# Gate projections that leave PSUM by one copy, with their product on GpSimd

## The chip, the cores and the metric

The kernel runs on one core of a Trainium2 chip. Its five engines are TensorE (PE; its weight loads are listed as PEld), VectorE (DVE), ScalarE (ACT), GpSimd (POOL) and SyncE (SP), which issues nearly all DMAs here. Each engine works through its own queue in order and waits on semaphores of the others. The metric is the device time of one execution in microseconds; less is better.

## The reference

One encoder layer over two sequences (1024 and 256 tokens, 1280 in all, width 1024). A wide projection feeds three groups of heads: a bidirectional gated delta rule (6 heads), bidirectional retention (6 heads) and windowed attention (4 heads). The output of each group is multiplied by a gate, silu of a slice of the projection, and the result goes through an output projection and a gated embedding.

```python
xn = rms_norm(h, norm_g)
proj = jnp.matmul(xn, w_in).astype(f32)
(a_qkv, a_gate, a_beta, a_alpha, b_q, b_k, b_v, b_gate,
 c_q, c_k, c_v, c_gate) = jnp.split(proj, splits, axis=-1)
...
o_a = (rms_norm(o_fwd + o_bwd, dn_norm_g) * jax.nn.silu(heads(a_gate, A_HEADS))).reshape(b, t, A_WIDTH)
...
o_b = head_layer_norm(r, ret_norm_g.astype(f32)) * jax.nn.silu(b_gate)
o_c = window_attention(...) * jax.nn.silu(c_gate)
mix = jnp.concatenate([o_a, o_b, o_c], axis=-1).astype(h.dtype)
h = h + jnp.matmul(mix, w_out)
h = h + jnp.matmul(p_i, w_ple) * jax.nn.sigmoid(jnp.matmul(h, w_pg))
```

silu(z) is z times sigmoid(z). There are eight gate slices of 128 columns: 0 to 2 for the delta rule, 3 to 5 for retention, 6 and 7 for attention.

## The kernel before

Activations stand transposed (features on partitions, tokens along the free axis), each as a high and a low part (`xh`, `xl`), and so do weights (`whi`, `wlo`). A dense product of 128 columns (`dense`, line 170) is three matmuls per 128 rows of the contraction and 256 tokens; it runs in three blocks of 512, 512 and 256 tokens. Each block fills one PSUM tile `mm`, of which there are two, and is then emptied by an evacuation function. `load_w` (line 133) brings a product's weights by one DMA (`raw`), rounds them on ScalarE (`whi`, line 148) and subtracts on GpSimd (`wlo`); the weights of the next product are loaded while one runs.

After the normalisation and the convolution of the delta rule comes the preparation (`prep_stream`, line 564). It goes through the ten token blocks from the last to the first and makes two steps for each, one per direction: 20 steps. A step takes Gram matrices (`sa`) from `kq`, decay factors from VectorE (`gt`), two matmuls `sb`, exponentials on ScalarE (`ge`), and products on VectorE (`at`, `l2`) and GpSimd (`l2`). Each step stores `at` (to `agd` and `ad`) and `l2` (to `l2d`). There are two `at` buffers, and ScalarE's copy into `at` (line 603) waits for the earlier stores. After five blocks, and again after ten, `invert` loads `agd` into `ot`, inverts 120 triangular 32x32 blocks for both directions by 61 operations on VectorE (`ot<-ot`, 120 partitions), and stores them as `yd`.

Beside the preparation run eleven dense products in the order cq0, cq1, gate 6, 7, 3, 4, 0, 5, cv, gate 1, 2 (`PP`). For a gate, the evacuation `evg` (line 468) computes sigmoid by three activations on ScalarE (exponential of the negated PSUM block, logarithm with bias one, exponential), then VectorE multiplies by the PSUM block. Gates 6 and 7 stay in `ot`; the other six go to DRAM (`gd`) by a DMA on SP's queue and are read again much later.

```python
sg = o if n >= 6 else gp.tile([128, 512], F32, tag="sg", name=nm("sg"))[:, :w]
sigmoid(sg, pp[:, :w])
tt(V, sg, sg, pp[:, :w], MUL)
```

Next come the product ck (`kst`), windowed attention, the joins of the inverted blocks (`join`: loads `an` and `yn`, GpSimd makes `yc`), the scan over 20 chunks (`scan_stream`), retention, and from about 830 us on the output products. `bias` is attention's table of distances, made on VectorE and finished by two selections on GpSimd.

The order of instructions on each engine is set at build time: a scheduler replays the program on a modelled timeline and writes one list per engine. Evacuations and weight roundings have high priority there. Pools on the right side of SBUF are a stack: `wp` (weights), `gp` (gate tiles, two of `sg`), `pc` (constants), and after `pc` closes, `sc` and `inv` for the scan and the joins.

Of the kernel before, what the change touches and what calls it, by code (L numbers as in the profile page):

```python
# [8 lines left out]
F32 = mybir.dt.float32  # L9
# [43 lines left out]
def encoder_kernel(ctx: ExitStack, tc: tile.TileContext, I, O, dbg=None, upto=99):  # L53
# [3 lines left out]
    def nm(s):  # L57
        uid[0] += 1
        return f"{s}_{uid[0]}"
# [14 lines left out]
    wp_cm = tc.tile_pool(name="wp", bufs=2, side="right")  # L74
    wp = wp_cm.__enter__()
    gp_cm = tc.tile_pool(name="gp", bufs=2, side="right", reuse_waits="tile")
    gp = gp_cm.__enter__()
# [3 lines left out]
    def pt_(shape, name, dt=F32):  # L81
        return pc.tile(list(shape), dt, name=name)
# [4 lines left out]
    def tt(eng, out, a, b, op):  # L87
        eng.tensor_tensor(out=out, in0=a, in1=b, op=op)  # L88

    V, S, G = nc.vector, nc.scalar, nc.gpsimd  # L90
    MUL, ADD, SUB, MAX = ALU.mult, ALU.add, ALU.subtract, ALU.max
# [3 lines left out]
        name=nc.get_next_instruction_name(), act_func_set_id=ACT_SET, ins=[], outs=[]))  # L95

    def sigmoid(out, in_):

        S.activation(out=out, in_=in_, func=AF.Exp, scale=-1.0)
        S.activation(out=out, in_=out, func=AF.Ln, bias=one_c)  # L100
        S.activation(out=out, in_=out, func=AF.Exp, scale=-1.0)  # L101
# [85 lines left out]
    tmpp = tmp_cm.__enter__()  # L187
# [45 lines left out]
        return  # L233


    onesbd = pt_([128, 128], "onesbd")
    G.memset(onesbd, 0.0)
    for h in range(2):
        G.memset(onesbd[64 * h:64 * h + 64, 64 * h:64 * h + 64], 1.0)
# [12 lines left out]
    for d in range(2):  # L252
        sg = 1 if d == 0 else -1
# [130 lines left out]
    def plain(dst, eng=S, scale=None):  # L384
        def evac(p, t0, n):
            if scale is None:
                S.copy(dst[:, t0:t0 + n], p[:, :n])
            else:
                S.activation(out=dst[:, t0:t0 + n], in_=p[:, :n], func=AF.Copy, scale=scale)
        return evac  # L390
# [58 lines left out]
    def length(ns):  # L449
        return 12.8 * len(ns) or 1.0, prods(*ns)  # L450
# [15 lines left out]
    def product(n):  # L466
        if n in GCOL:
            def evg(pp, t0, w):
                o = ot[:, n, t0:t0 + w]
                sg = o if n >= 6 else gp.tile([128, 512], F32, tag="sg", name=nm("sg"))[:, :w]  # L470
                sigmoid(sg, pp[:, :w])
                tt(V, sg, sg, pp[:, :w], MUL)
                if n in GD:
                    nc.sync.dma_start(out=GD[n][:, t0:t0 + w], in_=sg)
                elif n < 3:
                    tt(V, o, o, sg, MUL)
            return [(GCOL[n], 128)], evg
        if n[0] == "c":

            return {"cq0": ([(3096, 64), (3224, 64)], plain(ot[:, 4, :], scale=cols[:, 54:55])),  # L480
                    "cq1": ([(3160, 64), (3288, 64)], plain(ot[:, 5, :], scale=cols[:, 55:56])),
                    "ck": ([(3352, 128)], evk),
                    "cv": ([(3480, 128)], plain(ot[:, 1, :]))}[n]
        p = int(n[1])
        col, dst = {"q": (1560, ot[:, 3 + p, :]), "k": (1944, kreg.get(p, ot[:, 0, :])), "v": (2328, ot[:, 1, :])}[n[0]]
        return [(col + 128 * p, 128)], plain(dst)
# [139 lines left out]
    if upto <= 3:  # L626
# [3 lines left out]
        wp_cm.__exit__(None, None, None)  # L630
        return

    pc_cm.__exit__(None, None, None)

    sp_cm = tc.tile_pool(name="sc", bufs=2, side="right", reuse_waits="tile")
    sp = sp_cm.__enter__()
# [433 lines left out]
    def fill():  # L1070
        nonlocal av
        yield from spread((10 * T_AT, attn_stream()), length(PB))
        cb_cm.__exit__(None, None, None)
        rc_cm, rt_cm, *r = ret_open()
        kv, av = ret_streams(*r)
        yield from prods(*RS[0])
        for p in range(3):
            yield from spread((13 * T_KV, kv(p)), length(RS[1 + 2 * p]))
            if p < 2:
                yield from spread((5 * T_AV, av(p)), length(RS[2 + 2 * p]))  # L1080

        raw = [a[:, 0:4 * GW].rearrange("p (k c) -> p k c", k=4) for a in (kreg[1], ot[:, 1, :])]
        for i in range(2):
            nc.sync.dma_start(out=raw[i], in_=I["w_out"][0][512 * i:512 * i + 512, 0:GW].rearrange("(k p) c -> p k c", p=128))
        yield from spread((5 * T_AV, av(2)), length(RS[6]))

        for _ in scan:
            pass
        for cm in (gp_cm, wp_cm):
            cm.__exit__(None, None, None)  # L1090
        fr = ctx.enter_context(tc.tile_pool(name="fr", bufs=1, reuse_waits="tile", side="right"))
        wraw.append(fr)
        wbuf.append(fr)
        wf.append(load_f(I["w_out"][0], 0, raw))
        with tc.tile_pool(name="fa", bufs=2, reuse_waits="tile") as fa:
            yield from weave((0.0, split_stream()), (0.0, fin_split(fa)))
        for cm in (rt_cm, rc_cm):
            cm.__exit__(None, None, None)
# [6 lines left out]
    for _ in weave((0.0, scan), (T_LEAD, fill())):  # L1105
        pass
# [14 lines left out]
    with tc.tile_pool(name="fw", reuse_waits="tile", bufs=2) as fw:  # L1121
# [5 lines left out]
        for gi, c0 in enumerate(GC):  # L1127
            w = wf.pop()
            wf.append(load_f(I["w_out"][0], GC[gi + 1]) if gi < 3 else load_f(I["w_pg"][0], 0))
            for b in (range(NB) if gi else FO):  # L1130
# [6 lines left out]
                if gi == 2:  # L1137

                    pp = fw.tile([128, 256], F32, tag="pp", name=nm("pp"), bufs=2)
# [19 lines left out]
        for gi, c0 in enumerate(GC):  # L1159
            w = wf.pop()  # L1160
# [48 lines left out]
```

## Time and profile before

| what | value |
|---|---|
| median of 3 runs | 1143.53 us (1140.28 to 1144.91) |
| profiled execution | 1143.9 us |
| its span | 1142.1 us |
| TensorE busy | 1044.9 us |
| VectorE busy | 663.0 us |
| ScalarE busy | 517.4 us |
| GpSimd busy | 394.6 us |
| first and last gate product | 234.6 and 431.2 us from the span's start |

In a row of the timeline the first numbers are start and length in microseconds, then engine, line, operation, output and inputs, and in brackets the idle time before it and what ended that. In a row of waits, the numbers are total time, times, and the longest. In a row of one tile's operations they are the shortest, median and longest duration in ns. In a row of a group: count, busy us and mean ns, then the idle time before it. `L88` and `L85` are lines of the helpers that record every elementwise operation and every matmul, so tile names tell these apart.

### The profile page before, as it was taken

What the parts mean: (1) busy time and instruction counts of PE and PEld (TensorE: products, weight loads), DVE (VectorE), ACT (ScalarE), POOL (GpSimd) and SP (SyncE); (2) the same over time, 40 slices, a digit from 0 to 9 for tenths busy, and PEclk for the clock granted to TensorE, in tenths of its full rate; (3) what the DMA queues carried; (4) which work ended last, traced back from release to release, by engine and by line L of the source; (5) the groups of instructions that cost most, each with busy time, mean ns of one, the idle gap of its engine ahead of it and who ended that gap; (6) DMA issues with size and microseconds to landing.
All of it is one profiled execution on the core that took longest, in us unless ns stands there. A gap on an engine that the chain in (4) does not pass through costs nothing. (4 is left out here: it accounts for less than half of the span.)

```text
span 1142.1 us, 25975 instructions
## 1 busy us (share of the span) xinstructions
PE 1044.9 (91%) x10345; PEld 957.7 (84%) x10345; DVE 663.0 (58%) x1321; ACT 517.4 (45%) x1184; POOL 394.6 (35%) x470
## 2 busy tenths in 40 slices
PE   6999989978697879899979999999789999999996
PEld 5989979978687869688869888888658999999996
DVE  6667667587888489456754565665865123411125
ACT  8575775666464322444534522323342012455554
POOL 3133333454342321223331434556362111224421
PEclk9999999999898989899988999999859999999999
DMA  7112202449544652562462443546557232101003
GB/s 244 38 43 60 61 20 60 115 131 217 148 121 137 151 132 53 100 143 72 104 161 65 110 103 103 142 122 177 137 152 231 85 111 84 47 1 48 11 38 148
DMA packets 196531, 120.63 MB, mean 106 GB/s; under 512 B 100266, under 2 KB 181338, under 8 KB 196410
## 3 DMA queue, kind: packets, MB, share of 16 engines
q1 hardware_dynamic: 196410, 118.97, 38.3%
q8 instruction: 82, 1.34, 0.5%
q14 instruction: 39, 0.32, 0.1%
HBM read 76.14 MB, written 42.78 MB: 104 GB/s over the span
## 5 line engine op out<-in xcount | busy, mean ns | idle before, releaser
L85 PE MATMUL mm<-xh,whi 128*128 128x256 f32 x1200 | 352.2, 294 | 38.9 <-DVE sg L88 29.7
L85 PE MATMUL mm<-xl,whi 128*128 128x256 f32 x1200 | 349.9, 292 | 0.0
L85 PE MATMUL mm<-xh,wlo 128*128 128x256 f32 x1200 | 347.0, 289 | 0.2 <-POOL wlo L88 0.2
L85 PEld LDWEIGHTS mm<-xh,whi 128*128 128x128 f32 x1200 | 233.9, 195 | 48.0 <-DVE sg L88 31.9
L85 PEld LDWEIGHTS mm<-xl,whi 128*128 128x128 f32 x1200 | 234.3, 195 | 3.4 <-issue 1.4
L85 PEld LDWEIGHTS mm<-xh,wlo 128*128 128x128 f32 x1200 | 233.8, 195 | 3.0 <-issue 0.9
L88 POOL TENSOR_TENSOR wlo<-raw,whi 128x1024 fp32r<-128x1024 f32 (+1 forms) x37 | 107.6, 2909 | 250.5 <-ACT whi L148 144.0
L88 DVE TENSOR_TENSOR ot<-ot 128x1284 f32<-128x1284 f32 (+16 forms) x131 | 99.5, 760 | 36.9 <-ACT ot L101 19.4
L85 PE MATMUL mm<-whi,xh 128*128 128x256 f32 x320 | 91.3, 286 | 2.4 <-DVE ot L88 2.4
L85 PE MATMUL sa<-whi,xh 128*128 128x256 f32 x320 | 91.2, 285 | 0.0
L85 PE MATMUL mm<-whi,xl 128*128 128x256 f32 x320 | 91.0, 285 | 0.0
L85 PE MATMUL mm<-wlo,xh 128*128 128x256 f32 x320 | 91.0, 285 | 0.0
L85 PE MATMUL sa<-whi,xl 128*128 128x256 f32 x320 | 90.8, 284 | 0.0
L85 PE MATMUL sa<-wlo,xh 128*128 128x256 f32 x320 | 90.6, 283 | 0.0
L520 DVE SCALAR_TENSOR_TENSOR ot<-ot,cols 128x1284 f32<-128x1284 f32 x36 | 76.1, 2115 | 23.0 <-ACT ot L515 22.3
L88 DVE TENSOR_TENSOR sgm<-sb,sgm 128x256 f32<-128x256 f32 x40 | 16.9, 423 | 94.8 <-ACT sgm L101 74.2
L85 PEld LDWEIGHTS mm<-whi,xh 128*128 128x128 f32 x320 | 61.1, 191 | 2.7 <-DVE ot L88 2.6
L88 POOL TENSOR_TENSOR ot<-ot,sgm 128x256 f32<-128x256 f32 x40 | 30.3, 760 | 88.9 <-DVE sgm L88 88.7
L85 PEld LDWEIGHTS mm<-wlo,xh 128*128 128x128 f32 x320 | 61.0, 191 | 0.0
L88 POOL TENSOR_TENSOR l<-kq,ge 64x384 f32<-64x384 f32 x40 | 48.1, 1203 | 37.3 <-ACT ge L595 30.5
L85 PEld LDWEIGHTS mm<-whi,xl 128*128 128x128 f32 x320 | 61.0, 190 | 0.0
L85 PEld LDWEIGHTS sa<-wlo,xh 128*128 128x128 f32 x320 | 60.8, 190 | 0.0
(288 smaller groups left out, 2185.0 us busy)
## 6 DMA issues: line engine op xcount, KB each, us to landing
raw<-in_w_in SPq DMA_DIRECT2D x28, 512.0 KB, 3.9
l2d<-l SPq DMA_DIRECT2D x20, 576.0 KB, 7.2
l<-l2d SPq DMA_DIRECT2D x40, 288.0 KB, 2.9
xt<-in_x_prompt SPq DMA_DIRECT2D x8, 512.0 KB, 6.6
x<-in_x_prompt SPq DMA_DIRECT2D x32, 128.0 KB, 2.1
raw<-in_w_pg SPq DMA_DIRECT2D x4, 1024.0 KB
yp<-ot SPq DMA_DIRECT2D x8, 512.0 KB, 2.6
ad<-at SPq DMA_DIRECT2D x20, 198.0 KB, 3.3
```

Source lines behind the costliest of these rows:

```text
L85: nc.tensor.matmul(out, lhsT, rhs, start=start, stop=stop)
L88: eng.tensor_tensor(out=out, in0=a, in1=b, op=op)
L520: V.scalar_tensor_tensor(out=Y[:, 0:1284], in0=R[:, j:j + 1284], scalar=cw(ti, j), in1=Y[:, 0:1284], op0=MUL, op1=ADD)
```

## The change

Each gate block is first copied from PSUM to an SBUF tile `sz` by ScalarE; the three activations start from `sz`, and the product of sigmoid and `sz` is on GpSimd. There is one `sz` tile. The pool `gp` closes at the end of the preparation, so that the pools of the scan come to lie where it was, and `onesbd`, a constant used only while others are made, moves to a temporary pool.

```diff
-    onesbd = pt_([128, 128], "onesbd")
+    onesbd = tmpp.tile([128, 128], F32, name="onesbd")
...
                 sg = o if n >= 6 else gp.tile([128, 512], F32, tag="sg", name=nm("sg"))[:, :w]
-                sigmoid(sg, pp[:, :w])
-                tt(V, sg, sg, pp[:, :w], MUL)
+                zt = gp.tile([128, 512], F32, tag="sz", name=nm("sz"), bufs=1)[:, :w]
+                S.copy(zt, pp[:, :w])
+                sigmoid(sg, zt)
+                tt(G, sg, sg, zt, MUL)
...
     pc_cm.__exit__(None, None, None)
+    gp_cm.__exit__(None, None, None)
...
-        for cm in (gp_cm, wp_cm):
-            cm.__exit__(None, None, None)
+        wp_cm.__exit__(None, None, None)
```

The scheduler makes a new order of it. Three places matter. The first is VectorE where the first inversion begins (`ot<-ot 120x...` is the inversion; `gt`, `ge`, `at`, `l2` are preparation steps; `ot_90<-ot_90,mm` and `sg` are gate products). Before:

```order
L88 TENSOR_TENSOR gt_310_3538<-ghl_374,mr1_343 128x768
L88 TENSOR_TENSOR ge_303_3478<-ge_303_3478,mr0_334 128x384
L88 TENSOR_TENSOR at_306_3488<-sa_298_3453,ge_303_3478 128x6x32
L88 TENSOR_TENSOR l2_307_3489<-sa_298_3453,ge_303_3478 64x3x64 x2
L88 TENSOR_TENSOR at_306_3488<-sa_299_3460,ge_303_3478 128x6x32
L88 TENSOR_TENSOR l2_307_3489<-sa_299_3460,ge_303_3478 64x3x64 x2
L88 TENSOR_TENSOR l2_307_3489<-kc_301_3471,ge_303_3478 128x6x64
L88 TENSOR_TENSOR ot_90<-ot_90,mm_281_3104 128x256
L88 TENSOR_TENSOR gt_325_3653<-ghl_374,mr0_334 128x768
L88 TENSOR_TENSOR ot_90<-ot_90 120x2x32x32
L88 TENSOR_TENSOR ge_311_3540<-ge_311_3540,mr1_343 128x384
L88 TENSOR_TENSOR sg_286_3194<-sg_286_3194,mm_285_3145 128x512
```

And of the changed kernel:

```order
L88 TENSOR_TENSOR ge_279_3021<-ge_279_3021,mr1_343 128x384
L88 TENSOR_TENSOR at_282_3031<-sa_261_2873,ge_279_3021 128x6x32
L88 TENSOR_TENSOR l2_283_3032<-sa_261_2873,ge_279_3021 64x3x64 x2
L88 TENSOR_TENSOR at_282_3031<-sa_262_2880,ge_279_3021 128x6x32
L88 TENSOR_TENSOR l2_283_3032<-sa_262_2880,ge_279_3021 64x3x64 x2
L88 TENSOR_TENSOR l2_283_3032<-kc_264_2891,ge_279_3021 128x6x64
L88 TENSOR_TENSOR ot_90<-ot_90 120x2x32x32
L88 TENSOR_TENSOR ot_90<-ot_90 120x2x30 x2
L88 TENSOR_TENSOR ot_90<-ot_90 120x2x58
L88 TENSOR_TENSOR ot_90<-ot_90 120x2x2x29
L88 TENSOR_TENSOR ot_90<-ot_90 120x2x84
```

Before, the eleventh step (its `ge` is the second row) stands ahead of the inversion, and steps and gate products stand between its operations. Now the tenth step is the last ahead of it, 28 operations of the inversion follow in one piece, and the ten remaining steps come after that, woven with the rest. On TensorE the `sb` matmuls of the eleventh to twentieth step move behind more dense matmuls accordingly.

The second place is SP's queue at the end of the preparation, where the first inversion's result `yd` is stored, the last two steps are stored (`agd0_0`, `agd1_0` and what follows them), and the second inversion is loaded (`ot_90<-agd`). Before:

```order
L614 DMA agd0_0_404<-at_394_4209 32x6x33 x4
L616 DMA ad0_0_400<-at_394_4209 128x2x198
L423 DMA yd0_1_409<-ot_90 3840x1x32
L423 DMA yd1_1_411<-ot_90 3840x1x32
L617 DMA l2d0_0_380<-l2_395_4210 128x2x576
L614 DMA agd1_0_406<-at_401_4290 32x6x33 x4
L399 DMA ot_90<-agd0_0_404 120x1056
```

And of the changed kernel:

```order
L423 DMA yd0_1_409<-ot_90 3840x1x32
L423 DMA yd1_1_411<-ot_90 3840x1x32
L616 DMA agd0_0_404<-at_412_4245 32x6x33 x4
L618 DMA ad0_0_400<-at_412_4245 128x2x198
L619 DMA l2d0_0_380<-l2_413_4246 128x2x576
L399 DMA ot_90<-agd0_0_404 120x1056
L616 DMA agd1_0_406<-at_419_4326 32x6x33 x4
```

`yd` has moved ahead of the stores of the last two steps.

The third place is GpSimd beside gates 1 and 2, in the changed kernel (`sg_426`, `sg_429`, `sg_432` are the three blocks of gate 1, `sg_438` is the first of gate 2; `yc` is the first join's, and `wlo_436` belongs to ck, two products on):

```order
L819 CAST qh_458_4942<-ot_90 64x256 x2
L88 TENSOR_TENSOR sg_426_4429<-sg_426_4429,sz_427_4430 128x512
L243 AFFINE_SELECT bias_4763<-bias_4763 128x384 x2
L88 TENSOR_TENSOR yc_487_5152<-yn_482_5080,mblk_4752 128x960
L88 TENSOR_TENSOR wlo_436_4560<-raw_434_4557,whi_435_4559 128x1024
L88 TENSOR_TENSOR sg_429_4498<-sg_429_4498,sz_430_4499 128x512
L88 TENSOR_TENSOR sg_432_4543<-sg_432_4543,sz_433_4544 128x256
L88 TENSOR_TENSOR sg_438_4612<-sg_438_4612,sz_439_4613 128x512
```

Gate 1's second product stands behind `bias`, `yc` and a weight subtraction. Before, GpSimd had no gate product there; `bias` and `yc` stood side by side as well.

## The prediction

> **What bounds the kernel now.** I read the page's first part, then the chain that ended last, then the busy time by stretch, the waits of 180 to 440 us, and last the timeline of each engine in that stretch.
>
> ```profile
> PE 1044.9 (91%) x10345; PEld 957.7 (84%) x10345; DVE 663.0 (58%) x1321; ACT 517.4 (45%) x1184; POOL 394.6 (35%) x470
> 225.00:289.70 64.70, 55.23 (x459) 50.77 (x459) 50.60 (x97) 40.51 (x92) 32.92 (x34) 0.95 0.74 181
> 289.70:382.70 93.00, 74.33 (x607) 70.67 (x608) 86.09 (x155) 45.80 (x96) 31.08 (x28) 0.91 0.45 127
> 382.70:432.00 49.30, 36.79 (x294) 36.38 (x293) 31.50 (x49) 14.35 (x24) 16.86 (x21) 0.90 0.59 145
> 432.00:870.00 438.00, 409.37 (x5122) 344.83 (x5121) 274.66 (x739) 164.79 (x438) 170.05 (x251) 0.92 0.46 121
> ```
>
> The first row says that TensorE sets the time: 1044.9 of 1142.1 us busy, and its work is not changed. So the change can only be worth TensorE's idle time and slow clock. The other rows are stretches with busy PE, PEld, DVE, ACT, POOL, then granted clock, DMA share and GB/s. All gates lie in the first three of them (207 us), where TensorE is idle 40.7 us. Call them stage 1 (gates 6 and 7), stage 2 (gates 3, 4, 0, 5 beside the first inversion) and stage 3 (gates 1 and 2). In stage 2 VectorE is busy 86.1 of 93.0 us: there it is nearly a second bound. From 432 us on TensorE is 93% busy, so a time won before it is carried to the end.
>
> ```profile
> PE mm L85 <- DVE sg L88: 29.7, 8, 11.6
> ACT at L603 <- DMA ad<-at: 39.9, 15, 8.3
> PE sb L85 <- DVE gt L88: 5.2, 4, 2.9
> 295.42 0.58 PE L85 MATMUL mm<-xh,whi 128*128 128x256 f32 x1 [5.73 <-DVE sg L88]
> 305.21 0.43 PE L85 MATMUL mm<-xh,whi 128*128 128x256 f32 x1 [2.94 <-DVE sg L88]
> 350.34 0.58 PE L85 MATMUL mm<-xh,whi 128*128 128x256 f32 x1 [6.14 <-DVE sg L88]
> 407.41 0.29 PEld L85 LDWEIGHTS mm<-xh,whi 128*128 128x128 f32 x1 [11.83 <-DVE sg L88]
> 284.80 0.28 PE L85 MATMUL mm<-xh,wlo 128*128 128x256 f32 x1
> 295.80 0.41 PE L85 MATMUL mm<-xl,whi 128*128 128x256 f32 x1
> ```
>
> TensorE's largest wait of 180 to 440 us is 29.7 us, eight times, on the gate product `sg`: it is the last reader of the PSUM buffer that a later block of matmuls needs. Three such waits are in stage 2 (14.8 us), the longest (11.6) in stage 3. After such a wait matmuls take 0.41 us instead of 0.28, so each costs some 1.5 us more (estimate: a dozen matmuls by 0.13).
>
> **The change, part by part.** PSUM first.
>
> ```profile
> L99 ACT ACTIVATE sg<-mm x18: 375/597/601, 284.0 to 427.3; 128x512 f32<-128x512 f32 x12, 128x256 f32<-128x256 f32 x6
> L88 DVE TENSOR_TENSOR sg<-sg,mm x18: 399/680/689, 294.7 to 431.2; 128x512 f32<-128x512 f32 x12, 128x256 f32<-128x256 f32 x6
> L88 DVE TENSOR_TENSOR ot<-ot,mm x6: 420/686/687, 234.6 to 282.9; 128x512 f32<-128x512 f32 x4, 128x256 f32<-128x256 f32 x2
> L387 ACT COPY ot<-mm x3: 367/587/588, 379.7 to 385.3; 128x512 f32<-128x512 f32 x2, 128x256 f32<-128x256 f32 x1
> ```
>
> It adds 24 copies on ScalarE, 16 by 0.587 and 8 by 0.367 = 12.3 us, at the place where the first exponential stood. ScalarE is half idle in stage 2 (45.8 of 93.0) and its cover is that idle time; without it the 12.3 us would delay the same queue's `ge` exponentials and `at` copies. With the copy, the buffer is free 0.6 us after the block ends, in place of after three activations and VectorE's queue. Taken alone that removes the stage 2 waits, 14.8 us and three slow starts (4.5).
>
> But the same stage has VectorE's bound, and the matmuls `sb` of each preparation step wait for its `gt`. What does VectorE's load become?
>
> ```profile
> L88 DVE TENSOR_TENSOR sg<-sg,mm 128x512 f32<-128x512 f32 x8 | 5.5, 682 | 4.8 <-ACT sg L101 4.7
> L88 DVE TENSOR_TENSOR sg<-sg,mm 128x256 f32<-128x256 f32 x4 | 1.6, 412 | 0.1
> L88 POOL TENSOR_TENSOR elw<-er,ehw 128x512 fp32r<-128x512 f32 x4 | 5.2, 1291 | 9.0 <-ACT ehw L1165 6.5 <-issue 2.5
> L88 POOL TENSOR_TENSOR ot<-ot,sgm 128x256 f32<-128x256 f32 x40 | 30.3, 760 | 88.9 <-DVE sgm L88 88.7
> L88 POOL TENSOR_TENSOR kq<-ot,rr 128x512 f32<-128x512 f32 x12 | 23.3, 1947 | 38.0 <-ACT rr L541 38.0
> L88 POOL TENSOR_TENSOR kq<-ot,rr 128x256 f32<-128x256 f32 x6 | 9.1, 1524 | 3.8 <-ACT rr L541 3.8
> 323.25 2.81 POOL L88 TENSOR_TENSOR wlo<-raw,whi 128x1024 fp32r<-128x1024 f32 x1 [17.39 <-ACT whi L148]
> 323.71 3.15 DVE L88 TENSOR_TENSOR gt<-ghl,mr 128x768 fp32r<-128x768 f32 x1
> 351.21 0.96 DVE L88 TENSOR_TENSOR gt<-ghl,mr 128x768 fp32r<-128x768 f32 x1
> ```
>
> Out of stage 2 go twelve products (5.5 + 1.6 = 7.1) and the 4.8 us that VectorE waited for their exponentials: 11.9 us less. In come twelve products on GpSimd, whose price is not in the trace for this form: 1.29 and 0.76 us by the nearest rows (two SBUF inputs, same size), 13.4 us; 1.95 and 1.52 by the `kq` rows, 21.7 us. That is more than VectorE's 7.1, and it is not free for VectorE: beside a GpSimd subtraction of 2.81 us its `gt` took 3.15 us, clear of one 0.96, so 2.2 of 2.8 us were lost. How much of the new GpSimd time VectorE loses is between none and all; I take half, 6.7 us, since its operations that read PSUM seem untouched and some of the time GpSimd will be the one that waits. Last, VectorE's new order has one preparation step fewer ahead of the inversion, and for 28 operations nothing but the inversion: that step, some 4.8 us (estimate: 43.2 us of the nine steps' rows in stage 2 over nine), falls out of an idle place into the busy one. Sum: -11.9 + 6.7 + 4.8 = -0.4 us. **The preparation ends where it ended**, within -7.1 (nothing lost) and +14.6 (21.7 lost). TensorE, with its 14.8 us no longer spent on `sg`, then stands ahead of the preparation and waits for `gt` and `ge`; the order lets it do dense blocks first, but no further than the last step. Of stage 2's 19 us I count nothing as gained.
>
> The Trainium skill (SBUF — State Buffer, "Who interferes with whom") says that a VectorE instruction with two SBUF inputs and a GpSimd instruction that reads SBUF exclude each other for the whole instruction, and that one with a single SBUF input does not contend. The pair of rows above agrees. By that rule the old product (one input from PSUM) was free of it, the new one never is, and the rule speaks against the change: with every product blocking in full, the preparation would end 6.3 us later instead of 0.4 earlier, and the result would be that much worse.
>
> Stage 1 has no wait on the product; there `at` waits for its stores (39.9 us in all) set the pace. Six products leave VectorE, six come to a GpSimd busy 32.9 of 64.7 us: 0, within 3 either way.
>
> Stage 3 is where I expect the gain.
>
> ```profile
> 379.71 5.41 SPq L423 DMA_DIRECT2D yd<-ot  x2
> 385.23 3.99 SPq L617 DMA_DIRECT2D l2d<-l  x1
> 389.32 2.42 SPq L614 DMA_DIRECT2D agd<-at  x4
> 381.14 0.36 DVE L88 TENSOR_TENSOR at<-sa,ge 128x192 f32<-128x192 f32 x1
> 395.82 0.60 ACT L99 ACTIVATE sg<-mm 128x512 f32<-128x512 f32 x1 [2.94 <-PE mm L85]
> 402.35 3.82 DVE L88 TENSOR_TENSOR ot<-ot 120x2048 f32<-120x2048 f32 x1 [9.37 <-DMA ot<-agd]
> 406.67 0.69 DVE L88 TENSOR_TENSOR sg<-sg,mm 128x512 f32<-128x512 f32 x1
> 407.25 1.79 POOL L88 TENSOR_TENSOR yc<-yn,mblk 128x960 f32<-128x960 f32 x1
> 417.93 0.60 ACT L99 ACTIVATE sg<-mm 128x512 f32<-128x512 f32 x1 [3.47 <-PE mm L85]
> ```
>
> Gate 1's first product ran at 406.67 only, behind the inversion's first operation, which waited for a load; so TensorE stood from 395.5 to 407.4, and gate 2's second block could start at 417.9. Afterwards TensorE goes on with gate 1's third block (24 matmuls, 2.9 us) and gate 2's first (5.9): 404.4. For the next block it needs gate 1's third copy, which needs the one `sz` tile, which is held by gate 1's second product, which stands on GpSimd behind `yc`, a wait for the load `yn`, and a `wlo`. Behind that copy on ScalarE stand `sz`, `sg` and the next `whi`. When does `yc` run? In the old order the stores `yd` (5.4 us) and `l2d` (4.0) stood between the last step's `at` (done 381.5) and its store (389.3); in the new order `yd` goes out ahead of the last two steps. Up to 7.8 us of the queue's time are saved; I take 6. So `yc` at 401.3, + 1.8, + `wlo` 2.5, + product 1.3, + copy 0.6 = 407.5 against 417.9: **10.4 us gained**, at least 4.4 (nothing saved on the queue), at most 13.5 (TensorE itself, 404.4).
>
> The tiles of the scan now lie where the gates' tiles were, and their loads stand behind the last gate's store (431.6 us before). The scan's first matmul ran at 486.5:
>
> ```profile
> 431.63 0.32 SPq L474 DMA_DIRECT2D gd<-sg  x1
> L85 PE MATMUL sa<-vt,yc x48: 218/218/267, 486.5 to 780.1; 64*64 64x64 f32 x48
> ```
>
> 55 us of cover, so 0; without it, the loads' few us would delay the scan. Behind each gate store on SP's queue stand `at` stores and weight loads; a product that ends later delays them by as much, which is in the bounds. `onesbd` in the temporary pool: 0. The order after 660 us is unchanged; a reordered scan, 0 within 3.
>
> Sum: 0 - 0.4 - 10.4 + 0 = -10.8 us. The profiled execution took 1143.9 us (its span 1142.1), 0.4 above the median of 1143.53: 1133. A measurement of this kernel can tell about 0.5%, 5.7 us, from no change.
>
> **The rivals.**
>
> *TensorE gets it all.* If VectorE loses little to GpSimd and the preparation ends 7 us earlier, TensorE keeps nearly all of the 29.7 us and the slow starts (6), less a stall of 3 to 7 that stays in stage 3: about -29, 1115. For it: the new order puts dense work ahead of the steps. Against it: VectorE's 86 of 93.
>
> *Slower: GpSimd blocks VectorE.* The products cost what `kq` cost and block in full: the preparation ends 14.6 later. All of stage 3 hangs on that end, so 10.4 turns into 4 lost, and TensorE, waiting for `gt` step by step, starts slow twice more (3): 1151. It decides from a loss of some 17 us of VectorE's time on. For it: 2.2 of 2.8 lost in the pair of rows. Against it: half of GpSimd's time in stage 2 is idle now.
>
> *The wait only changes its name.* With one `sz` tile, each copy waits for the product before it, and the copy stands behind `at` copies that wait up to 8.3 us for stores. Then PSUM is freed hardly sooner: 1143. Against it: copy, three activations and product are 0.6 + 0.6 + 0.7 + 0.6 + 1.3 = 3.8 us, below a block's 5.9.
>
> **How the numbers follow.** The forecast 0.48 (its own range 1127 to 1141), all of it 0.17, slower 0.15, renamed 0.20. Faster by over 0.5% (below 1138): most of the first (0.40) and the second, 0.57. Within: 0.08 of the first and 0.18 of the last, 0.26. Slower: 0.17. The range goes from near the second case, 1116, to 1149, short of the slower one.
>
> **What would show it.** Right: TensorE's waits on `sg` gone; a wait on the third copy of gate 1 left, 3 to 7 us, behind `yc`; TensorE's waits on `gt` or `ge` grown by some 15 us in stage 2; the preparation's last `l` near 382 us; the inversion's last-half load sooner by about 6 us. Wrong: TensorE waits little in stage 2 (first rival), or VectorE's `gt`, `ge` and `ot` groups grown by over 15 us beside GpSimd (second), or waits on ScalarE's copy as long as those on `sg` were (third).

## The result, and the profile after

The changed kernel takes 1149.19 us (median; 1146.24 to 1150.67) against 1141.42 us of the kernel before on the same chip: ratio 1.0061, 95% interval 1.004 to 1.0082. It is slower by 0.6%, where 0.9% faster was forecast. The profiled execution took 1150.47 us, with a span of 1148.8 us (before 1142.1). A few executions of some versions were disturbed and much longer than the others; they are left out of every ratio below, and of e16 no other execution was traced.

First the page's busy row:

```profile
PE 1042.9 (91%) x10345; PEld 959.0 (83%) x10345; DVE 666.8 (58%) x1297; ACT 531.3 (46%) x1208; POOL 426.2 (37%) x494
```

Then stretches of the changed kernel: stages 2 and 3, and one from 225 us to the end of the preparation's last `l`. Columns: us, then busy PE, PEld, DVE, ACT, POOL, granted clock, DMA share, GB/s.

```profile
289.70:382.70 93.00, 68.21 (x547) 64.70 (x547) 89.57 (x128) 50.67 (x105) 49.24 (x40) 0.88 0.40 118
382.70:432.00 49.30, 39.66 (x305) 39.06 (x304) 30.29 (x54) 17.98 (x34) 17.68 (x17) 0.85 0.63 146
225.00:398.20 173.20, 137.62 (x1113) 129.20 (x1114) 147.08 (x233) 97.64 (x208) 90.58 (x82) 0.91 0.52 139
```

The last one in the kernel before, where the last `l` ended at 382.7:

```profile
225.00:382.70 157.70, 129.56 (x1066) 121.44 (x1067) 136.69 (x251) 86.31 (x188) 64.00 (x62) 0.92 0.57 149
```

In stage 2 TensorE does less (68.2 us in place of 74.3), though its waits on `sg` are gone, and VectorE is busier (89.6 in place of 86.1), though twelve products left it. Over the longer stretches VectorE is busy 147.1 us in place of 136.7. The last `l` ends 15.5 us later: 10.4 of it VectorE's busy time, 5.1 its idle time.

Where does VectorE's extra busy time come from? The view by groups, 180 to 480 us (us busy, mean ns of one | idle ahead). After, and then the same groups of before:

```profile
L88 DVE TENSOR_TENSOR ot<-ot 120x60 f32<-120x60 f32 (+16 forms) x125 | 105.7, 846 | 24.7 <-DMA ot<-agd 21.0 <-ACT ot L101 0.9
L88 DVE TENSOR_TENSOR l<-sa,ge 64x192 f32<-64x192 f32 x80 | 28.0, 350 | 0.5
L88 DVE TENSOR_TENSOR gt<-ghl,mr 128x768 fp32r<-128x768 f32 x18 | 23.9, 1326 | 0.1
L88 DVE TENSOR_TENSOR ge<-ge,mr 128x384 f32<-128x384 f32 x20 | 20.1, 1004 | 12.8 <-ACT ge L597 12.8
L88 DVE TENSOR_TENSOR l<-kc,ge 128x384 f32<-128x384 f32 x20 | 19.6, 982 | 0.8 <-ACT kc L585 0.2
```

```profile
L88 DVE TENSOR_TENSOR ot<-ot 120x60 f32<-120x60 f32 (+16 forms) x125 | 89.5, 716 | 18.3 <-DMA ot<-agd 14.8 <-ACT ot L101 0.9
L88 DVE TENSOR_TENSOR l<-sa,ge 64x192 f32<-64x192 f32 x80 | 28.0, 350 | 0.6
L88 DVE TENSOR_TENSOR gt<-ghl,mr 128x768 fp32r<-128x768 f32 x18 | 25.3, 1408 | 0.2
L88 DVE TENSOR_TENSOR ge<-ge,mr 128x384 f32<-128x384 f32 x20 | 17.2, 860 | 8.3 <-ACT ge L595 8.1
L88 DVE TENSOR_TENSOR l<-kc,ge 128x384 f32<-128x384 f32 x20 | 14.5, 725 | 1.2 <-ACT kc L583 0.7
L88 DVE TENSOR_TENSOR sg<-sg,mm 128x512 f32<-128x512 f32 (+1 forms) x18 | 10.7, 592 | 4.9 <-ACT sg L101 4.7
```

The four groups with two SBUF inputs (inversion `ot<-ot`, `gt`, `ge`, `l<-kc`) take 169.3 us in place of 146.5: **22.8 us more for the same number of instructions**, more than twice the 10.7 us of `sg` products that left. The group `l<-sa`, whose one input lies in PSUM, took 28.0 us in both. This sum, "the four groups", is used below.

The waits of 180 to 440 us:

```profile
PE sb L85 <- DVE gt L88: 18.5, 6, 10.7
PE mm L85 <- ACT sz L472: 13.1, 5, 9.6
ACT sz L472 <- POOL sg L88: 17.3, 6, 9.8
```

And the timeline where the order changed, with the last `l` and the first operations on `kst`, the evacuation of ck, which follows the last gate (in brackets idle time and its releaser). Two rows of the kernel before stand behind it:

```profile
290.46 27.75 DVE L88 TENSOR_TENSOR ot<-ot 120x2048 f32<-120x2048 f32 x28 [11.02 <-DMA ot<-agd]
318.13 0.95 DVE L88 TENSOR_TENSOR gt<-ghl,mr 128x768 fp32r<-128x768 f32 x1
319.23 0.66 PE L85 MATMUL sb<-gt,la 128*128 128x384 f32 x1 [10.71 <-DVE gt L88]
396.41 1.82 DVE L88 TENSOR_TENSOR l<-kc,ge 128x384 f32<-128x384 f32 x1
424.08 24.21 DVE L88 TENSOR_TENSOR ot<-ot 120x168 f32<-120x168 f32 x31
440.59 0.58 ACT L463 CAST kst<-mm 64x512 fp32r<-64x512 f32 x1
448.32 0.68 DVE L88 TENSOR_TENSOR kst<-mm,kst 64x512 fp32r<-64x512 f32 x1
```

```profile
289.66 3.83 DVE L88 TENSOR_TENSOR ot<-ot 120x2048 f32<-120x2048 f32 x1 [5.45 <-DMA ot<-agd]
433.27 0.58 ACT L463 CAST kst<-mm 64x512 fp32r<-64x512 f32 x1 [4.58 <-PE mm L85]
```

The 29.7 us on `sg` have become 13.1 us on the copy, and the 5.2 us on `gt` have become 18.5. VectorE stands 11.0 us before the inversion, whose load has not come (5.5 before the change), then does 28 of its operations in one piece, and TensorE waits 10.7 us for the next step's `gt`. ScalarE's first copy into `kst` is the mark for the end of the gates on TensorE, since it reads ck's first block. It came at 433.27 before and comes at 440.59 now, 7.3 us later, and the span grew by 6.7: the whole loss is made ahead of it. VectorE's first `kst` operation (435.65 before, 448.32 now) is no such mark. It is 12.7 us later because it stands behind 31 operations of the second inversion.

Stage 3, from the timeline:

```profile
418.03 1.84 POOL L88 TENSOR_TENSOR yc<-yn,mblk 128x960 f32<-128x960 f32 x1 [11.64 <-DMA yn<-yd]
419.84 2.33 POOL L88 TENSOR_TENSOR wlo<-raw,whi 128x1024 fp32r<-128x1024 f32 x1
422.13 1.29 POOL L88 TENSOR_TENSOR sg<-sg,sz 128x512 f32<-128x512 f32 x1
423.46 0.37 ACT L472 COPY sz<-mm 128x256 f32<-128x256 f32 x1 [9.80 <-POOL sg L88]
423.88 0.58 PE L85 MATMUL mm<-xh,whi 128*128 128x256 f32 x1 [9.64 <-ACT sz L472]
```

That is the chain the forecast named, link by link, 16 us later than it said.

### The profile page after: what moved, and what is told of

Read it like the earlier page. It is cut to its first block, busy times and chain, and to the rows that moved or that the text cites. A ratio compares the mean times of both kernels' runs of the same rounds, so it can differ in the third digit from the quotient of the medians.

```text
span 1148.8 us, 25993 instructions
## 1 busy us (share of the span) xinstructions
PE 1042.9 (91%) x10345; PEld 959.0 (83%) x10345; DVE 666.8 (58%) x1297; ACT 531.3 (46%) x1208; POOL 426.2 (37%) x494
## 4 chain that ended last, share of the span: by engine, by line
PE 58%; DVE 18%; DMA 9%; ACT 6%; issue 4%; SPq 3%; POOL 1%; DVEq 0%; ACTq 0%; POOLq 0%
PE mm L85 29%; PE sa L85 15%; DVE ot L88 8%; PE sb L85 7%; PE tr L85 3%; DVE ot L522 3%; DMA ad<-at 2%; SPq L616 1%; DMA agd<-at 1%; DVE l L88 1%; DMA ot<-agd 1%; PE tr L842 1%; DMA yd<-ot 1%; PE tr L1154 1%; ACT ge L597 1%
## 5 line engine op out<-in xcount | busy, mean ns | idle before, releaser
L85 PE MATMUL mm<-xh,whi 128*128 128x256 f32 x1200 | 351.5, 293 | 26.4 <-ACT sz L472 13.4
L88 DVE TENSOR_TENSOR ot<-ot 128x1284 f32<-128x1284 f32 (+16 forms) x131 | 115.8, 884 | 43.2 <-DMA ot<-agd 21.0
L522 DVE SCALAR_TENSOR_TENSOR ot<-ot,cols 128x1284 f32<-128x1284 f32 x36 | 76.1, 2115 | 23.1 <-ACT ot L517 22.3
L85 PEld LDWEIGHTS sa<-whi,xh 128*128 128x128 f32 x320 | 60.7, 190 | 0.4 <-DVE gt L1027 0.4
```

What stands on the lines that cost most here:

```text
L85: nc.tensor.matmul(out, lhsT, rhs, start=start, stop=stop)
L522: V.scalar_tensor_tensor(out=Y[:, 0:1284], in0=R[:, j:j + 1284], scalar=cw(ti, j), in1=Y[:, 0:1284], op0=MUL, op1=ADD)
```

## The experiments

Three theories. **Blocking**: GpSimd's products take VectorE's time. **Order**: the inversion's piece on VectorE stands ahead of a step it used to follow. **One tile**: the copy waits for the product before it. Ratios are to the kernel before, from runs on the same chip.

**e1, the products left out.**

```diff
                 sigmoid(sg, zt)
-                tt(G, sg, sg, zt, MUL)
```

> The 24 products are left out (copy and sigmoid stay), so GpSimd loses some 27 us of work in the preparation, while VectorE's order still has the inversion's 28 operations in one piece ahead of nine or ten preparation steps. Blocking theory (GpSimd's products take VectorE's time): the piece of 28, 27.75 us in the changed kernel, falls to 21 to 23 us, the preparation's last l, 398.2 us there, ends at 384 to 388, and the time is 1134 to 1142. Order theory (the piece ahead of the steps delays them, whatever GpSimd does): the piece shrinks little, the last l stays at 393 to 398, time 1145 to 1150. One-tile theory (the copy waits for the product before it): the last l changes little, but the second block of gate 2 starts 8 us earlier, time about 1142.

1137.17 us, ratio 0.995 (0.9929 to 0.997); the last `l` ended at 383.4. VectorE's order is nearly the same, with a similar wait for the load, 13.0 us in place of 11.0:

```profile
286.70 23.95 DVE L88 TENSOR_TENSOR ot<-ot 120x2048 f32<-120x2048 f32 x28 [12.97 <-DMA ot<-agd]
```

The four groups took 146.2 us. So the products cost VectorE 169.3 - 146.2 = 23.1 us and the kernel 1.1%, in an otherwise nearly equal order. Blocking, with the time it named; the piece itself shrank less than it said (23.95 against 21 to 23), since `wlo` and `l` still stand beside it. The 1.1% is not blocking alone: without the product, the copy's waits on it (17.3 us on ScalarE) are gone as well.

**e2, the product on VectorE, copy and one tile kept.**

```diff
-                tt(G, sg, sg, zt, MUL)
+                tt(V, sg, sg, zt, MUL)
```

> The copy out of PSUM and its one tile are kept, the product goes back to VectorE (two SBUF inputs in place of one PSUM and one SBUF). VectorE's order is woven again: steps and inversion alternate. Blocking theory: VectorE gets 7 to 9 us of products back but loses less to GpSimd: the last l at 383 to 388, time 1135 to 1142. Order theory: the same end, 1135 to 1142, so this run only says whether the product's engine or the copy and the pools made the loss. Pools theory (the early closing of the gates' pool and the scan's tiles in it made the loss): 1147 to 1151.

Ratio 1.0023 (1.0004 to 1.0043), last `l` at 384.0. The last `l` came where blocking said, but the gain in time that both theories named (ratio under 1) did not appear: a miss for both. The eighteen `sg` products, now with two SBUF inputs, took 14.8 us in place of 10.7 (in e18, with most of GpSimd's two-input work gone, the same eighteen took 10.8):

```profile
L88 DVE TENSOR_TENSOR sg<-sg,sz 128x512 f32<-128x512 f32 (+1 forms) x18 | 14.8, 825 | 9.8 <-ACT sg L101 9.8
```

**e3, the steps first; e4, the pools alone.** e3 wraps a preparation step in high priority; twelve steps then stand ahead of the piece, in place of ten (counted by `ge`; the expectations count `gt`, of which one or two more stand ahead). e4 is the kernel before with the change's `onesbd` and pool edits only.

```diff
+                    hp = tc.high_priority()
+                    hp.__enter__()
                     gt = pa.tile([128, 2, 6, 64], F32R, tag="gt", name=nm("gt"), bufs=1)
 ...
+                    hp.__exit__(None, None, None)
                     yield T_PREP / 2
```

> The changed kernel, with the preparation's steps at high priority: the inversion's long piece on VectorE comes three steps later (after fourteen in place of eleven), all work is the same and the products stay on GpSimd. Order theory: TensorE's wait of 10.7 us for gt of the twelfth step goes, the last l ends 5 to 10 us earlier (388 to 393), time 1140 to 1145. Blocking theory: what GpSimd takes from VectorE stays taken, the piece is only met later: the last l within 3 us of 398, time 1147 to 1151.

> Only the pools part of the change: onesbd in the temporary pool, the gates' pool closed behind the preparation, everything else as before. Pools theory: 1146 to 1150, with the scan's first matmul some 20 us later than before (486.5). Blocking and order theories: 1140 to 1143, no change.

e3: ratio 1.0042 (1.0027 to 1.0057), last `l` at 380.7, the wait for the load down to 1.8 us, the four groups at 161.9. The last `l` came 17.5 us earlier, more than the order theory asked, and the time moved 0.2%, less than it asked: the last `l` alone does not set the time. e4: 1.0013 (1.0 to 1.0026): the pools alone do not make the 0.6%, though up to 0.3% is not excluded.

**e5, no products and steps first.** Both edits, e1's and e3's.

> The 24 products are left out and the preparation's steps have high priority: the fourth corner of a square with the changed kernel (last l of the preparation at 398.2), the one without products (383.4) and the one with steps first (380.7). If GpSimd's products and the order are two separate losses, they add: 398.2 - 14.8 - 17.5 = 366, within 4, and the time is 1130 to 1135. If they are one loss (the products only hurt inside the long piece of the inversion that stands ahead of the steps), the last l is at 376 to 381 and the time 1137 to 1142.

1127.9 us, ratio 0.9884 (0.9857 to 0.9911); last `l` at 372.9, between the two expectations, and the time below both. Without products the order is worth 0.7%, with them 0.2% with overlapping intervals: the two losses do not simply add.

**e6, the disputed cost by itself.** Nothing of the kernel, only VectorE's operations `vo` alone and beside GpSimd's `go`.

```diff
+    def v2(i):
+        tt(V, vo[i % 4], va, vb)
+    def vp(i):
+        tt(V, vo[i % 4], va, pa)
+    def g2(i):
+        tt(G, go[i % 4], ga, gb)
+    phase(v2, 40, None, 0)
+    phase(None, 0, g2, 10)
+    phase(v2, 40, g2, 10)
+    phase(vp, 40, g2, 10)
 ...
```

> Nothing of the kernel is left: VectorE runs 40 additions of 128x512 (two SBUF inputs, then one PSUM and one SBUF input, then copies with one SBUF input), alone and beside ten GpSimd additions of 128x512, sixteen GpSimd copies or 24 GpSimd memsets. Blocking theory, in full: 40 two-input additions take 24 to 28 us alone and 12 to 13 us more beside the ten GpSimd additions; those with a PSUM input, and the copies, take no longer than alone. Blocking by half, as the forecast had it: 6 to 7 us more. No blocking (the loss is order alone): within 1 us. GpSimd's memset, which reads nothing, costs VectorE nothing by the blocking theory.

The timeline, in order VectorE alone, GpSimd alone, both, VectorE's PSUM form beside GpSimd and alone, and VectorE beside memsets; `va`, `vb` lie in SBUF, `pa` in PSUM:

```profile
6.90 24.17 DVE L63 TENSOR_TENSOR vo<-va,vb 128x512 f32<-128x512 f32 x40
32.55 12.73 POOL L63 TENSOR_TENSOR go<-ga,gb 128x512 f32<-128x512 f32 x10
47.38 34.69 DVE L63 TENSOR_TENSOR vo<-va,vb 128x512 f32<-128x512 f32 x40
46.70 16.77 POOL L63 TENSOR_TENSOR go<-ga,gb 128x512 f32<-128x512 f32 x10
84.24 24.00 DVE L63 TENSOR_TENSOR vo<-va,pa 128x512 f32<-128x512 f32 x40
196.02 24.00 DVE L63 TENSOR_TENSOR vo<-va,pa 128x512 f32<-128x512 f32 x40
169.75 24.17 DVE L63 TENSOR_TENSOR vo<-va,vb 128x512 f32<-128x512 f32 x40
```

Forty additions take 24.17 us alone and 34.69 beside ten GpSimd additions: 10.5 us lost for 12.73 us of GpSimd's time, **0.83**, while GpSimd loses 4.0 itself. With one input in PSUM VectorE loses nothing (84.24 beside them, 196.02 alone, both 24.00), nor beside GpSimd's memsets (169.75). So a 128x512 product that costs VectorE 0.60 us costs it some 1.05 us when GpSimd does it (0.83 by 1.27). By the Trainium skill (SBUF — State Buffer, "Who interferes with whom") VectorE operations with two SBUF inputs and GpSimd operations that read SBUF shut each other out, and one that reads PSUM for its second input does not; these rows agree.

**e7 and e8, the products split between the engines.** e7 has those of stage 2 on VectorE and the others on GpSimd, e8 the reverse.

```diff
-                tt(G, sg, sg, zt, MUL)
+                tt(V if n in (0, 3, 4, 5) else G, sg, sg, zt, MUL)
```

> The changed kernel with the products of gates 3, 4, 0 and 5 (stage 2) on VectorE, and those of gates 6, 7, 1 and 2 on GpSimd. Blocking theory (the loss is made where VectorE is the bound): last l at 380 to 386, time 1138 to 1143. Rival (the products of stages 1 and 3 make the loss, through the queue behind yc): time 1146 to 1150.

> The counterpart: products of gates 3, 4, 0 and 5 on GpSimd, those of gates 6, 7, 1 and 2 on VectorE. Blocking theory: the whole loss is there, last l at 392 to 399, time 1146 to 1150. Rival (stages 1 and 3 make the loss): last l at 385 to 390, time 1140 to 1144.

e8: 1.0079 (1.0047 to 1.011), last `l` at 395.1, both as blocking said. e7: 1.0049 (1.0034 to 1.0064): a miss. Its order again has ten steps ahead, and the last `l` ended at 388.3. Since both halves lose, the two runs do not place the loss, and blocking in stage 2 alone does not explain e7.

**e9 and e10, two copy tiles.** The room comes from small constants (`sumid`, `mrbd`, `onesbd`, `nea`, part of `rvb`) that move into `ot[:, 7]`, free until gate 7, and `onesR` into a buffer that is free until the preparation. e9 has the product on GpSimd, e10 on VectorE.

```diff
-                zt = gp.tile([128, 512], F32, tag="sz", name=nm("sz"), bufs=1)[:, :w]
+                zt = gp.tile([128, 512], F32, tag="sz", name=nm("sz"), bufs=2)[:, :w]
...
-    sumid = pt_([128, 24], "sumid")
+    sumid = ot[:, 7, 512:536]
...
-        t2 = pt_([128, 128], f"mrbd{d}")
+        t2 = ot[:, 7, 256 + 128 * d:384 + 128 * d]
```

> The changed kernel with two copy tiles in place of one (the room is made by small constants that move into a part of the output tile which is free until the gates); VectorE's order keeps its piece of 28 (here 32) ahead of nine steps, the products stay on GpSimd. One-tile theory (the copy waits for the product before it, and holds ScalarE's queue): ScalarE's 17.3 us of waits of the copy on the product go, the preparation's last l ends 5 to 8 us earlier (390 to 393), time 1141 to 1145. Blocking theory: the waits go, but VectorE's time is as lost as before: last l 395 to 400, time 1146 to 1150.

> The same two copy tiles, with the product on VectorE. With one tile this ended at ratio 1.0023, with 29.5 us of ScalarE's copies waiting for the product. One-tile theory: these waits fall below 8 us, the last l ends at 376 to 382, time 1131 to 1138: this is what the early release of PSUM alone is worth. Rival (the release is worth nothing, since VectorE sets the end of stage 2): last l 383 to 386, time 1140 to 1144.

e9: 0.998 (0.9966 to 0.9995), last `l` at 391.0. e10: 0.9941 (0.9919 to 0.9963), last `l` at 382.5. This looked like the one tile. It needed the control below.

**e11 and e12, the kernel before with other edits.** e11 moves `wlo` and the preparation's two `l<-kq` products from GpSimd to VectorE, with the gates untouched; e12 is e3's edit on the kernel before.

```diff
-            tt(G, lo, raw, hi.bitcast(F32), SUB)
+            tt(V, lo, raw, hi.bitcast(F32), SUB)
...
-                        tt(G, l2[lr, :, :, h, :], kq[lr, :, 1, tb].rearrange("p q (c t) -> p c q t", c=2), ge[lr, 1], MUL)
+                        tt(V, l2[lr, :, :, h, :], kq[lr, :, 1, tb].rearrange("p q (c t) -> p c q t", c=2), ge[lr, 1], MUL)
```

> The kernel before, its gates untouched, with two other GpSimd operations moved to VectorE: the weights' low part wlo (2.4 us each on GpSimd) and the preparation's two l products of each step (1.4 us each). In stage 2 some 5 wlo and 18 l, 37 us of GpSimd time. Blocking in full (0.83 of GpSimd's time lost to VectorE, as measured alone): VectorE gives 31 us back and takes on 5 x 1.25 + 18 x 0.56 = 16: the last l ends some 10 to 15 us earlier (368 to 373), time 1128 to 1136. Blocking by half: 18 back, 16 on: no change, 1139 to 1144. No blocking: 16 us later, 1148 or more.

> The kernel before, with the preparation's steps at high priority, as control: its order had thirteen steps ahead of the inversion already, and has as many now. Both theories: within 0.3% of before, 1139 to 1144. If the priority alone is worth several us, what it did for the changed kernel says nothing on the order there.

e11: the four groups fell from 146.5 to 113.8 us and the last `l` ended at 349.0, 34 us earlier, though VectorE took on more work: blocking at its clearest. Yet the time was 0.9981 (0.9965 to 0.9998), a miss. TensorE then waited 22.1 us for one evacuation (`cv` into `ot`, shown for e18), so the first `kst` copy came only 9.7 us earlier, and these were lost again behind it, for a reason that is open. e12: 0.9993 (0.9971 to 1.0015), as said.

**e13 and e14, the controls: constants moved as above, one tile,** the product on GpSimd in e13 and on VectorE in e14.

> Control for the two copy tiles: the small constants moved in the same way, but one copy tile, product on GpSimd. One-tile theory: as slow as the changed kernel, 1146 to 1150, against 1140.7 with two tiles. Rival (the moved constants made the gain): 1139 to 1142.

> The same control with the product on VectorE. One-tile theory: 1143 to 1147 (ratio 1.002, as with the constants unmoved), against 1136.2 with two tiles. Rival (the moved constants made the gain): 1135 to 1138.

e13 is the changed kernel with nothing but the constants moved: 1132.26 us, **ratio 0.9902** (0.9879 to 0.9924). That is faster than either theory allowed and faster than with two tiles, and 1.6% from the changed kernel's 1.0061. e14, with the product on VectorE: 1.0062 (1.0031 to 1.0094), slower than either theory allowed and slower than with two tiles. The second tile made the one 0.8% slower and the other 1.2% faster, so these runs give it no price. e13 has eleven steps ahead of the inversion, then a piece of 31, and its loads left SP 8 to 9 us earlier. Its timeline, and the changed kernel's rows for the same loads behind it:

```profile
267.81 0.36 SPq L398 DMA_DIRECT2D ot<-agd  x1
276.64 0.35 SPq L398 DMA_DIRECT2D ot<-agd  x1
281.39 4.11 DVE L88 TENSOR_TENSOR ot<-ot 120x2048 f32<-120x2048 f32 x1 [1.77 <-DMA ot<-agd]
418.94 0.58 ACT L462 CAST kst<-mm 64x512 fp32r<-64x512 f32 x1 [2.51 <-PE mm L85]
```

```profile
276.74 0.36 SPq L399 DMA_DIRECT2D ot<-agd  x1
284.44 0.35 SPq L399 DMA_DIRECT2D ot<-agd  x1
```

The inversion starts 9.1 us earlier (281.39 against 290.46), and the four groups take 159.6 us, 9.7 less, probably since fewer of GpSimd's operations fall beside VectorE's. The first `kst` copy comes 21.7 us earlier.

**e15 and e16, on the version with two tiles and the product on VectorE:** e15 adds the steps first, e16 adds e11's edits.

> Two copy tiles, product on VectorE, and the preparation's steps at high priority. Order theory: TensorE's 18.6 us of waits for gt fall below 10, time 1131 to 1135, ratio 0.989 to 0.992. Rival (order is worth nothing by itself, as it was worth 0.2% with one tile and GpSimd's product): 1135 to 1138.

> Two copy tiles, product on VectorE, and also the weights' low part and the preparation's two l products on VectorE. Blocking theory (GpSimd's two-input operations cost VectorE 0.83 of their time): the preparation's last l ends 25 to 35 us earlier (345 to 357), and TensorE's waits for gt go: 1128 to 1134. Rival (the preparation's end is not what sets the time once the steps are early; the inversion and the evacuation of cv behind it are): last l early all the same, time 1134 to 1139.

e15: 0.993 (0.9906 to 0.9955), not told apart from e10; its waits for `gt` were 12.5 us, not below 10. e16: 1129.2 us, 0.9864 (0.9841 to 0.9887), in the time that blocking named, and the fastest version that computes everything. The end of its last `l` is not known.

**e17 and e18, the last two.** e17 is the kernel before with the constants moved; e18 has e15's and e16's edits together.

> The kernel before with the same small constants moved, and nothing else (twelve steps ahead of the inversion in place of thirteen, woven as before). Order theory: the constants are worth only what the preparation starts earlier, 2 to 4 us: 1138 to 1143, ratio 0.996 to 1. Rival (the moved constants make the gain by themselves): ratio 0.987 to 0.992, 1129 to 1135.

> Two copy tiles, the gates' product, the weights' low part and the preparation's two l products on VectorE, and the preparation's steps at high priority. Blocking theory: VectorE's inversion, gt, ge and l groups run at their clear times (the inversions' 122 operations at 71 to 73 us in place of 100.7 in the changed kernel), the last l ends at 338 to 352, and the time is 1124 to 1130. Rival (with the products off GpSimd the order of the scan sets what is left): last l early, time 1130 to 1138.

e17: 0.9962 (0.9943 to 0.998). So in the kernel with moved constants the change is a gain: 0.9902 against 0.9962, about 0.6%, where it is a loss of 0.6% with the constants in their old place. e18: 0.9898 (0.9875 to 0.9921), 1132.02 us, slower than blocking asked, within its rival, though its four groups are at 113.8 us. Its longest waits on the way to `kst`:

```profile
PE mm L85 <- ACT ot L386: 31.0, 1, 31.0
ACT ot L386 <- DVE ot L420: 22.4, 1, 22.4
```

TensorE waits once, 31.0 us, for the evacuation of `cv` into `ot`, which waits for the last operation of the first inversion.

The versions that are compared most, with the four groups, the start of the first copy into `kst` and the rest of the span behind it (ratios from the timed runs, the last three columns from the profiled ones). With the constants moved and in e18, the four groups hold one operation of 128x1284 (some 1.7 us) less, and in some one `gt` more. In e1, e2, e5, e9, e10 and e18 ScalarE was busy right ahead of the copy, so TensorE may have been some us earlier:

| version | product | tiles | steps ahead | ratio | four groups | first `kst` copy | rest |
|---|---|---|---|---|---|---|---|
| before | VectorE, PSUM | none | 11 | 1 | 146.5 | 433.3 | 708.8 |
| e17: constants moved | VectorE, PSUM | none | 11 | 0.9962 | 146.0 | 427.1 | 709.4 |
| after | GpSimd | 1 | 10 | 1.0061 | 169.3 | 440.6 | 708.2 |
| e3 | GpSimd | 1 | 12 | 1.0042 | 161.9 | 424.8 | 718.9 |
| e9: moved | GpSimd | 2 | 10 | 0.9980 | 162.8 | 420.8 | 717.0 |
| e13: moved | GpSimd | 1 | 11 | 0.9902 | 159.6 | 418.9 | 715.3 |
| e2 | VectorE | 1 | 11 | 1.0023 | 148.4 | 428.1 | 712.2 |
| e14: moved | VectorE | 1 | 10 | 1.0062 | 151.5 | 427.3 | 723.7 |
| e10: moved | VectorE | 2 | 10 | 0.9941 | 150.9 | 425.5 | 706.4 |
| e18: moved | VectorE | 2 | 12 | 0.9898 | 113.8 | 418.8 | 714.1 |
| e1 | none | 1 | 10 | 0.9950 | 146.2 | 413.7 | 718.4 |
| e5 | none | 1 | 12 | 0.9884 | 148.6 | 408.1 | 717.5 |

## Why the prediction was wrong

The forecast's parts and what the two profiled executions show for them, in us:

| part | forecast | measured |
|---|---|---|
| stage 1, to the first inversion's start | 0 | +0.8 |
| stage 2, from there to the last `l` | -0.4 | +14.7 |
| stage 3, from there to the first `kst` copy | -10.4 | -8.2 |
| the scan and the rest | 0 | -0.6 |
| sum | -10.8 | +6.7 |

*The step that failed is the sum of stage 2*, -11.9 + 6.7 + 4.8 = -0.4, "The preparation ends where it ended". VectorE from the first inversion's start to the last `l` (length, busy time, granted clock, DMA): before, after, and e1, which has the copy and the order but no products:

```profile
289.66:382.70 93.04, 86.13 (x155) 0.91 0.45 127
290.46:398.23 107.77, 99.91 (x153) 0.87 0.44 121
286.70:383.45 96.75, 88.37 (x153) 0.93 0.50 134
```

e1 parts the miss of 15.1 us in two. *First, blocking*, the 6.7 us of "I take half". From e1 to the changed kernel stage 2 grows by 11.0 us and VectorE's busy time in it by 11.5, for the eleven products that stand there, 11.9 us at 1.28 and 0.74: nearly all of it. By itself it was 0.83 (e6). In the whole preparation it is 22.8 us (23.1 against e1) for 16 products of 1.28 and 8 of 0.74, 26.4 us together: 0.86. So 6.7 should have been 11. The reason given for half, that GpSimd would often be the one that waits, is true (16.77 against 12.73 us in e6) and does not help VectorE: the time that the one waits is time in which the other works, and nearly the sum of the two passes (24.17 + 12.73 = 36.9 alone, 34.69 together).

*Second, and larger, the terms -11.9 and +4.8.* Without any product they promised 7.1 us less; e1 took 3.7 more. VectorE's idle time should have fallen from 6.9 to 2.1 us and was 8.4 in e1 and 7.9 in the changed kernel: the 4.7 us that it waited for the gates' exponentials went, and waits for the steps' own exponentials `ge` came in their place. The waits within stage 2, of before, of e1 and of the changed kernel, and of the last the `sb` matmuls of the last step:

```profile
DVE sg L88 <- ACT sg L101: 4.7, 3, 2.4
DVE ge L88 <- ACT ge L596: 5.8, 2, 4.8
DVE ge L88 <- ACT ge L597: 5.4, 3, 4.1
391.02 0.51 PE L85 MATMUL sb<-gt,la 128*128 128x384 f32 x2
```

The longest, 4.1 us, is the last step's. Its `gt` was done at 384.8, but its `sb` ran at 391.02 only, since a dense block stood ahead of it in TensorE's new order; `ge` followed.

Busy time should have fallen to 83.8 us and was 88.4 in e1, where the inversion's 61 operations took 47.6 us in place of 41.7. Probably more of GpSimd's `wlo` and `l` fell beside them in the new order, since over the whole preparation the four groups of e1 are no longer than before. The step that falls behind was 4.8 us by its rows; that it would cost no more than its rows was assumed.

*The price of a product was right*: the `elw` row said 1.29 and 0.76; twelve of the sixteen large ones took 1.26 to 1.30, and four of the eight small ones 0.73 or 0.74. The copies too: 0.585 and 0.373 us against 0.587 and 0.367. TensorE's waits on `sg` went, and those on `gt` grew by 13.3 us, near the "some 15".

*Stage 1, nothing within 3*: the inversion started at 290.46 against 289.66: right.

*Stage 3* had the mechanism right (`yn`, `yc`, `wlo`, product, copy) and the base wrong: 407.5 + 15.5 = 423.0, measured 423.88. Behind the last `l`, `yc` came 24.6 us later before and 19.8 now, so 4.8 of the 6 us taken for the queue were saved. But the base had moved by 15.5, and the gain of 10.4 us became a loss of 5.9 for gate 2's second block (417.93 before).

*The scan, 0 within 3*: its first matmul came 22 us later and its last (`sa<-r,yc`) at 828.0 against 823.5; behind the first `kst` copy the span is 0.6 us shorter. The size was right here, in part by luck: over all versions that rest lies between 706 and 724 us, though of its instructions only `wlo` was changed, and that in e11, e16 and e18 alone. The versions that came to `kst` early mostly have the longer rest. What sets it was not tried and stays open.

*The rivals.* "GpSimd blocks VectorE" came nearest (14.6 us later, 1151), and its sign, the `gt`, `ge` and `ot` groups grown by over 15 us, came (17.7): its blocking in full was about right, its price of a product (the `kq` rows) wrong, so its 14.6 is luck in part. "The wait only changes its name" did happen (13.1 us on the copy, 17.3 of ScalarE's on the product), but the runs give it no sign.

*What the forecast did not weigh at all* is that the order is not a detail beside the terms. The changed kernel and e13 hold the same work for the preparation and differ by 1.6%; the change costs 0.6% with the constants in one place and gains 0.6% with them in the other. Blocking is shown (e1, e6, e11). That a mere move of constants decides the sign is shown too (e13 and e17). That it does so by the new order, and by which of its places, is only argued. In e13 the inversion starts 9.1 us earlier, stage 2 is 5.1 us shorter (102.7 against 107.8), and 7.5 us more come between the last `l` and `kst`. An early start alone need not bring anything: in e17 the inversion starts 9.8 us earlier than before (279.87), the four groups are the same, and the last `l` ends at 382.5, where it was.

A rival that no run excludes is the granted clock. Its mean over the timed runs was 0.946 in the changed kernel, 0.952 in e13 and 0.945 in e14, and 0.940 in e11 against 0.950 in the kernel before beside it. In most versions the longer executions have the lower clock (e1: 1131.96 us at 0.953, 1142.01 at 0.943). Whether it is a cause of the differences between versions or goes along with them is not shown.

## What to carry to other kernels

Work with two SBUF inputs is not unloaded from VectorE by giving it to GpSimd while VectorE has two-input work of its own: VectorE lost 0.83 to 0.87 us for each us of it, that is some 1.05 us for a 128x512 product, more than the 0.60 us that it saved. An operand that stays in PSUM is safe from that, and the copy that frees the PSUM buffer takes this safety away. A wait that a change removes is saved only if no other takes its place: here 4.7 us on one set of exponentials became 5.4 on another. Where a scheduler sets the order, an edit's worth is only known within what a neutral edit moves: here that was 0.4% for the kernel before and 1.6% for the changed one.

## What was not expected of the hardware

A VectorE copy of 128x512 has one SBUF input only, and yet it was hit as hard: forty took 13.50 us alone and 24.03 beside ten GpSimd additions, 10.5 us lost again. The Trainium skill (SBUF — State Buffer, "Who interferes with whom") says that copies can take a mode with two ports, which contends; the rows agree. The prediction's shorter wording, that one SBUF input does not contend, leaves this condition out. The rows are e6's, beside the additions and alone:

```profile
110.40 24.03 DVE L86 COPY vo<-va 128x512 f32<-128x512 f32 x40
222.18 13.50 DVE L86 COPY vo<-va 128x512 f32<-128x512 f32 x40
```

Before the change, VectorE already lost some 31 us of the preparation to GpSimd's `wlo` and `l`, more than this change added: the four groups took 146.5 us and in e11 113.8, where the window holds one operation of 1.7 us less.
